# Weight tiles of 1024 columns instead of 512 in a hybrid decoder step

## The chip, the cores and the metric

The kernel runs on one core of one Trainium2 chip. The metric is the device time of one execution in microseconds. A core has five engines that run side by side, each with its own queue in fixed order: TensorE (PE, matrix products; PEld is its weight load), VectorE (DVE), ScalarE (ACT), GpSimd (POOL) and SyncE (SP, which here issues the DMA transfers). They meet through semaphores, and a waiting instruction holds up everything behind it on its engine.

## The reference

One layer of a decoder is computed in fp32 for 1024 prompt tokens and for 8 sample tokens, each of which has a cache of 4096 earlier keys and values in pages of 128. The core of it:

```python
def swiglu(h, w_gate, w_up, w_down):
    return (jax.nn.silu(h @ w_gate) * (h @ w_up)) @ w_down
...
h = x + 0.5 * swiglu(rmsnorm(x, p['ffn1_norm']), p['ffn1_w_gate'], p['ffn1_w_up'], p['ffn1_w_down'])
z = rmsnorm(h, p['mix_norm']) @ p['w_in']
xq, xf, xi, xg, dq, dk, dv = jnp.split(z, IN_SPLITS, axis=-1)
o_hg, s_new = hgrn2_mixer(xq, xf, xi, xg, lb, s0, p['hg_out_norm'])
...
o = jnp.concatenate([o_hg.reshape(B, L, HG_WIDTH), o_da.reshape(B, L, DA_WIDTH)], axis=-1).astype(dt)
h = h + o @ p['w_out']
y = h + 0.5 * swiglu(rmsnorm(h, p['ffn2_norm']), p['ffn2_w_gate'], p['ffn2_w_up'], p['ffn2_w_down'])
```

The model width is 1024, the FFN's inner width 2816. `o_hg` is a gated linear recurrence over chunks of 64 tokens (4 heads), `o_da` an attention of two softmax maps per head (4 heads), for the prompt over itself and for the sample tokens over their cache.

## The kernel before

**Products in three passes.** A product is made at fp32 precision from parts in a faster format: each operand is split into a high part H (the value cast to fp32r) and a low part L (the value less H), and H·H, H·L and L·H are added up in PSUM. So every weight passes through the chain of `split` (L105 and L106): a DMA brings a raw tile `wr` of 512 columns, ScalarE casts it into `wH`, and VectorE, or GpSimd, subtracts to get `wL`. A profile shows all three steps of a weight under L106 (cast and subtraction) and L354 (the load); the tokens' own splits (`xn`, `h`) have L106 too and are told apart by the tile's name.

**Weights in tiles.** The host lays the weights out in blocks of 128 x 512. `wtile` (L359) asks for all that one product needs: two blocks for a gate, up or output matrix of 128 columns (8 row blocks), four for 256 columns of the input projection, and two for 256 columns of the down projection (one in its first block of rows). Raw tiles have 4 buffers, `wH` and `wL` 7 each. `wload` (L350) is issued at a high priority. While the flag `shared[1]` is set, which is from the second token group's first half to the end of the first group's second half, every second tile's low part (`WPOOL`) is subtracted on GpSimd.

**Stages.** The tokens go in two groups of 512 (the sample tokens pass the first half with the first group and the second half with the second). The first group's FFN1 and input projection run alone, then the sample tokens' attention over the cache begins beside them. The second group's first half has the first group's mixer (recurrence, then attention) and the cache attention woven in (`weave`); the first group's second half (output projection, FFN2) has the second group's mixer and the rest of the cache attention; the second group's second half runs alone. In the cache attention each page of keys is loaded (`kv`), multiplied on GpSimd (L954) and reduced on VectorE (L955); each page of values is scaled and added up, for even pages on VectorE (L1004), for odd ones on ScalarE (L1006) and GpSimd (L1008).

**What sets the order.** The code is written in woven order, and a scheduler then sorts every engine's instructions by priorities and by a simulated run. The queues are fixed before the kernel starts. FFN steps that the prediction names: a gate product's result is multiplied by the norm's factor (L399) and, with its tanh, by itself (L402), the up product's result is multiplied in (L409), the factor once more on GpSimd (L411), and the sum is split for the down projection (L431, L433). L402 reads two SBUF tiles in the first group's second half and one SBUF tile and one PSUM bank in the second group's first.

Of the kernel before, what the change touches and what calls it, by code (L numbers as in the profile page):

```python
# [18 lines left out]
P = 128  # L19
# [3 lines left out]
EPS = 1e-6  # L23
# [5 lines left out]
# columns of the constant table  # L29
# [4 lines left out]
def shape_constants():  # L34
# [5 lines left out]
    for l in range(7):  # L40
# [6 lines left out]
        # the columns of right halves alone  # L47
# [12 lines left out]
def kernel(ctx: ExitStack, tc: tile.TileContext, I, O):  # L60
# [74 lines left out]
    def load_consts():  # L135
# [3 lines left out]
        # lower bound: c1n = -(1 - lb) / 2 with lb the softmax over the two rows  # L139
        l0 = DT("wr", [P, 512], bufs=4)  # L140
        l1 = DT("wr", [P, 512], bufs=4)
        SP.dma_start(l0, I["hg_lb_logits"][0:1].broadcast_to([P, 512]))
        SP.dma_start(l1, I["hg_lb_logits"][1:2].broadcast_to([P, 512]))
        mx = DT("wr", [P, 512], bufs=4)
# [8 lines left out]
        # lambda  # L153
        lv = DT("wr", [P, 512], bufs=4)
# [10 lines left out]
        # gains of the mixers  # L165
# [18 lines left out]
    # rows of the sample tokens  # L184
# [15 lines left out]
    class Group:  # L200
        """tokens that pass the weights together: tiles as wide as the group"""
# [9 lines left out]
    class Slice:  # L211
        """columns of a group that one matrix product takes"""
# [53 lines left out]
    def norm_sums(sl):  # L266
        """sums of squares by block, down the partitions; the columns of each height"""
# [6 lines left out]
    def norm_spread(sl, R, r):  # L274
        """the factors along a row, on all partitions"""
# [23 lines left out]
    def scaled(gi, sl, d):  # L299
        """what norm_finish makes, but for the norm's factors: those come with the products' results"""  # L300
# [6 lines left out]
    def norm_row(sl):  # L307
        """the factors alone, along a row"""
# [26 lines left out]
    def xn_pair(w):  # L335
        """room for high and low parts: in one tile, or one each"""
        t = DT("xn", [P, 528], F32R, bufs=17)
        if w <= 264:
            return t[:, 0:w], t[:, 264:264 + w]
        return t[:, 0:w], DT("xn", [P, 528], F32R, bufs=17)[:, 0:w]  # L340
# [9 lines left out]
    def wload(H, L, raw, src):  # L350
        # while DVE has the most to do, some of the low parts on Pool
        shared[0] += 1
        with hp():
            SP.dma_start(raw, src)  # L354
# [4 lines left out]
    def wtile(src, c):  # L359
        """c columns of weights, from tiles of 512 / c blocks of rows: pairs of (high, low) parts"""  # L360
        out = []
        for i in range(src.shape[0]):
            raw = DT("wr", [P, 512], bufs=4)
            H = DT("wH", [P, 512], F32R, bufs=7)
            L = DT("wL", [P, 512], F32R, bufs=7)
            wload(H, L, raw, src[i])
            out += [(H[:, k:k + c], L[:, k:k + c]) for k in range(0, 512, c)]
        return out

    def mm3(ps, W, sl):  # L370
        """ps = W^T x, weights stationary, in three passes"""
# [7 lines left out]
    FB = [2, 4, 4, 4, 4, 4]  # L379

    def ffn(pre, slices, done, deferred=False):
        wg, wu, wd = (I[pre + n] for n in ("_w_gate", "_w_up", "_w_down"))

        def gateup(f, hs):
# [30 lines left out]
            # by slices where what comes before goes by slices  # L415
# [104 lines left out]
    def evac(name, c, ps, tb, kind, row, factors):  # L520
        # of the norm: the factor, half of it, and the eps that it makes of EPS and of 64 EPS
# [15 lines left out]
        else:  # L537
# [9 lines left out]
            with tc.high_priority():  # L547
                if name == "aq":
                    # the scale of the scores over each head's slope comes with the norm
# [6 lines left out]
        # where it goes  # L556
# [15 lines left out]
        else:  # L572
# [3 lines left out]
            # high and low parts side by side, and so below each other once transposed  # L576
# [43 lines left out]
    def hgrn_head(b):  # L620
        """the logarithms of the decays"""
# [8 lines left out]
    def hgrn_block(b):  # L630
# [30 lines left out]
        def stage1(h, q):  # L661
            """decays of four levels (the first of the first half: the running one), and both sides' factors"""
# [19 lines left out]
        def stage2(h, q):  # L682
# [11 lines left out]
            def right(t, l):  # L694
                """the columns of right halves at a level"""
# [72 lines left out]
    def att_scores(h, b, KT):  # L768
        """softmax weights of both maps, combined"""
# [490 lines left out]
```

## Time and profile before

| | |
|---|---|
| Time of the runs | 2474.95 us median of 3 (2472.2 to 2476.01) |
| Profiled execution | span 2471.9 us; no other time of this execution is shown |
| TensorE busy | 2304.7 us, 93% |
| VectorE busy | 1827.5 us, 74% |
| ScalarE busy | 1071.8 us, 43% |
| GpSimd busy | 999.5 us, 40% |
| DMA | 402.37 MB, 163 GB/s mean |

Busy shares are means over stages with different limits, so the table by stretch of time has to be read before any of them means something. An instruction's duration is from its start on the engine to its end; where two engines hinder each other, the one that stands shows a longer duration, not an idle time. So for each instruction its shortest or median duration is to be set against its mean.

### The profile page before, as it was taken

What the parts mean: (1) busy time and instruction counts of PE and PEld (TensorE: products, weight loads), DVE (VectorE), ACT (ScalarE), POOL (GpSimd) and SP (SyncE); (2) the same over time, 40 slices, a digit from 0 to 9 for tenths busy, and PEclk for the clock granted to TensorE, in tenths of its full rate; (3) what the DMA queues carried; (4) which work ended last, traced back from release to release, by engine and by line L of the source; (5) the groups of instructions that cost most, each with busy time, mean ns of one, the idle gap of its engine ahead of it and who ended that gap; (6) DMA issues with size and microseconds to landing.
All of it is one profiled execution on the core that took longest, in us unless ns stands there. A gap on an engine that the chain in (4) does not pass through costs nothing. (4 is left out here: it accounts for less than half of the span.)

```text
span 2471.9 us, 44310 instructions
## 1 busy us (share of the span) xinstructions
PE 2304.7 (93%) x15101; PEld 2079.1 (84%) x15101; DVE 1827.5 (74%) x3750; ACT 1071.8 (43%) x2465; POOL 999.5 (40%) x788
## 2 busy tenths in 40 slices
PE   7999999989998978989899879889798999999999
PEld 6999999989877866767888767677687889999999
DVE  6555657596799796798798997997987766555554
ACT  4322324435544434545554643434465554322222
POOL 4100101381176374474684673785756310100000
PEclk9999999999998998999899999999999999999999
DMA  4332334684466467576785773566755652332332
GB/s 137 90 95 83 112 91 125 183 286 139 130 217 205 134 213 230 165 234 215 239 280 145 243 236 114 186 211 202 235 173 182 183 170 94 90 95 91 90 95 74
DMA packets 273396, 402.37 MB, mean 163 GB/s; under 512 B 29641, under 2 KB 104650, under 8 KB 273170
## 3 DMA queue, kind: packets, MB, share of 16 engines
q1 hardware_dynamic: 273170, 399.54, 52.0%
q8 instruction: 119, 1.95, 0.3%
q14 instruction: 107, 0.88, 0.1%
HBM read 361.22 MB, written 38.21 MB: 162 GB/s over the span
## 5 line engine op out<-in xcount | busy, mean ns | idle before, releaser
L376 PE MATMUL mm<-xn,wH 128*128 128x256 f32 (+2 forms) x4800 | 1121.8, 327 | 19.4 <-DVE xn L106 5.7
L376 PEld LDWEIGHTS mm<-xn,wH 128*128 128x128 f32 x4800 | 808.6, 192 | 94.8 <-DVE xn L106 8.1
L376 PE MATMUL mm<-xn,wL 128*128 128x256 f32 (+2 forms) x2400 | 782.7, 326 | 1.4 <-DVE wL L106 1.4
L106 ACT CAST wH<-wr 128x512 fp32r<-128x512 f32 x672 | 409.3, 617 | 518.1 <-PE mm L376 275.3
L106 DVE TENSOR_TENSOR wL<-wr,wH 128x512 fp32r<-128x512 f32 x504 | 414.7, 825 | 163.8 <-ACT wH L106 132.8
L431 PE MATMUL mm<-h,wH 128*128 128x264 f32 (+2 forms) x2112 | 487.0, 324 | 7.3 <-DVE ft L409 4.7
L376 PEld LDWEIGHTS mm<-xn,wL 128*128 128x128 f32 x2400 | 461.1, 192 | 36.8 <-DVE wL L106 1.8
L954 POOL TENSOR_TENSOR kv<-kv,ss 128x512 f32<-128x512 f32 x256 | 371.2, 1459 | 145.3 <-DMA kv<-in_cache_k 127.1
L431 PEld LDWEIGHTS mm<-h,wH 128*128 128x128 f32 x2112 | 349.9, 190 | 38.4 <-DVE ft L409 5.8
L411 POOL TENSOR_TENSOR ft<-ft,acc 128x256 f32<-128x256 f32 (+1 forms) x110 | 101.5, 922 | 656.6 <-DVE ft L409 645.9
L431 PE MATMUL mm<-h,wL 128*128 128x264 f32 (+2 forms) x1056 | 340.5, 323 | 0.0
L498 PE MATMUL mm<-wH,xn 128*128 128x256 f32 (+1 forms) x1728 | 325.5, 286 | 7.2 <-ACT ez L527 2.5
L106 POOL TENSOR_TENSOR wL<-wr,wH 128x512 fp32r<-128x512 f32 x168 | 237.9, 1417 | 223.0 <-ACT wH L106 184.7
L1004 DVE SCALAR_TENSOR_TENSOR sacc<-kv,sS,sacc 128x128 f32<-128x128 f32 x480 | 283.5, 645 | 20.4 <-POOL sacc L1008 20.4
L498 PEld LDWEIGHTS mm<-wH,xn 128*128 128x128 f32 (+1 forms) x1728 | 259.4, 180 | 17.5 <-ACT ez L527 3.2
L1006 ACT ACTIVATE kv<-kv,sS 128x128 f32<-128x128 f32 x512 | 164.5, 391 | 210.3 <-DMA kv<-in_cache_v 161.2
L498 PE MATMUL mm<-wL,xn 128*128 128x256 f32 (+1 forms) x864 | 246.2, 286 | 1.0 <-DVE wL L106 1.0
L1008 POOL TENSOR_TENSOR sacc<-sacc,kv 128x512 f32<-128x512 f32 x128 | 185.6, 1450 | 117.9 <-issue 27.3
L433 DVE SCALAR_TENSOR_TENSOR xr<-mm,xr 128x264 f32<-128x264 f32 (+2 forms) x288 | 146.0, 511 | 91.4 <-PE mm L431 91.0
L431 PEld LDWEIGHTS mm<-h,wL 128*128 128x128 f32 x1056 | 200.2, 190 | 14.7
L955 DVE TENSOR_REDUCE sS<-kv 128x8 f32<-128x512 f32 x256 | 170.8, 673 | 37.2 <-POOL kv L954 36.8
L498 PEld LDWEIGHTS mm<-wL,xn 128*128 128x128 f32 (+1 forms) x864 | 155.2, 180 | 4.7 <-DVE wL L106 1.2
(219 smaller groups left out, 2409.0 us busy)
## 6 DMA issues: line engine op xcount, KB each, us to landing
kv<-in_cache_k SPq DMA_DIRECT2D x256, 256.0 KB
kv<-in_cache_v SPq DMA_DIRECT2D x256, 256.0 KB
wr<-in_ffn_w_gate SPq DMA_DIRECT2D x176, 256.0 KB
wr<-in_ffn_w_up SPq DMA_DIRECT2D x176, 256.0 KB
wr<-in_ffn_w_down SPq DMA_DIRECT2D x176, 256.0 KB
wr<-in_w_in SPq DMA_DIRECT2D x96, 256.0 KB
aq<-qt SPq DMA_DIRECT2D x64, 128.0 KB
wr<-in_w_out SPq DMA_DIRECT2D x32, 256.0 KB
```

What stands on the lines that cost most here:

```text
L106: return ACT.copy(H, src), (eng or DVE).tensor_tensor(out=L, in0=src, in1=H.bitcast(F32), op=ALU.subtract)
L376: PE.matmul(ps[:, :w], a, b[k][:, :w], start=k == 0 and j == 0, stop=k == n - 1 and j == 2)
L411: POOL.tensor_tensor(out=t, in0=t, in1=sl.acc, op=ALU.mult)
L431: PE.matmul(ps[:, :w], a[:, cs], b[:, :w], start=j == 0 and q == 0, stop=j == m - 1 and q == 2)
L433: DVE.scalar_tensor_tensor(out=sl.xr[d][:, :w], in0=ps[:, :w], scalar=0.25, in1=sl.xr[d][:, :w], op0=ALU.mult, op1=ALU.add)
L498: PE.matmul(ps[:tb, 0:256], a, b, start=k == 0 and j == 0, stop=k == KC - 1 and j == 2)
L954: POOL.tensor_tensor(out=kt, in0=kt, in1=qb, op=ALU.mult)
L955: DVE.tensor_reduce(out=Sb[:, i], in_=kt.rearrange("p (n d) -> p n d", d=64), op=ALU.add, axis=AX.X)
L1004: DVE.scalar_tensor_tensor(out=acc[:, hs], in0=vt[:, hs], scalar=w, in1=acc[:, hs], op0=ALU.mult, op1=ALU.add)
L1006: ACT.activation(vt[:, hs], vt[:, hs], AF.Copy, scale=w)
L1008: POOL.tensor_tensor(out=acc, in0=acc, in1=vt, op=ALU.add)
```

## The change

`wtile` takes the blocks of 512 columns in pairs: one DMA of 128 x 2 x 512 into a raw tile of 1024 columns, one cast and one subtraction over 1024. Where a product needs an odd block (the down projection's first block of rows), half a tile is used. Raw buffers become 2 of 1024, `wH` and `wL` 4 each of 1024. The count for GpSimd's turn (`shared[0]`) goes up once per tile as before, so once per 1024 columns. The few constants that borrow raw buffers take slices of the new ones. Comments are left out in the new file, and with the lines added at L140 and behind L368 later lines stand one, then three further down.

```diff
-        l0 = DT("wr", [P, 512], bufs=4)
-        l1 = DT("wr", [P, 512], bufs=4)
+        l0t = WR()
+        l0 = l0t[:, 0:512]
+        l1 = l0t[:, 512:1024]
...
-        mx = DT("wr", [P, 512], bufs=4)
+        mx = WR()[:, 0:512]
...
-        lv = DT("wr", [P, 512], bufs=4)
+        lv = WR()[:, 0:512]
...
     def wload(H, L, raw, src):
         shared[0] += 1
         with hp():
-            SP.dma_start(raw, src)
+            SP.dma_start(raw.rearrange("p (n c) -> p n c", c=512), src)
             split(H, L, raw, POOL if shared[1] and shared[0] % WPOOL == 0 else DVE)
...
     def wtile(src, c):
         out = []
-        for i in range(src.shape[0]):
-            raw = DT("wr", [P, 512], bufs=4)
-            H = DT("wH", [P, 512], F32R, bufs=7)
-            L = DT("wL", [P, 512], F32R, bufs=7)
-            wload(H, L, raw, src[i])
-            out += [(H[:, k:k + c], L[:, k:k + c]) for k in range(0, 512, c)]
+        for i in range(0, src.shape[0], 2):
+            m = min(2, src.shape[0] - i)
+            raw, H, L = (t[:, 0:512 * m] for t in (WR(), DT("wH", [P, 1024], F32R, bufs=4), DT("wL", [P, 1024], F32R, bufs=4)))
+            wload(H, L, raw, src[i:i + m].rearrange("n p c -> p n c"))
+            out += [(H[:, k:k + c], L[:, k:k + c]) for k in range(0, 512 * m, c)]
         return out
 
+    def WR():
+        return DT("wr", [P, 1024], bufs=2)
```

GpSimd's queue in the second group's first half, where it goes from the third sample token's keys to the fourth's. Numbers behind a name tell buffers apart: `ss512_7978` and `ss512_10261` are the third and the fourth token's queries before, `ss512_7449` and `ss512_9600` after. Before:

```order
L106 TENSOR_TENSOR wL_9740<-wr_9738,wH_9739 128x512
L954 TENSOR_TENSOR kv_10041<-kv_10041,ss512_7978 128x512
L1008 TENSOR_TENSOR sacc_8089<-sacc_8089,kv_9948 128x512
L954 TENSOR_TENSOR kv_10137<-kv_10137,ss512_7978 128x512
L954 TENSOR_TENSOR kv_10188<-kv_10188,ss512_7978 128x512
L106 TENSOR_TENSOR wL_9752<-wr_9750,wH_9751 128x512
L1008 TENSOR_TENSOR sacc_8089<-sacc_8089,kv_10086 128x512
L954 TENSOR_TENSOR kv_10264<-kv_10264,ss512_10261 128x512
```

After:

```order
L106 TENSOR_TENSOR wL_9115<-wr_9113,wH_9114 128x1024
L1011 TENSOR_TENSOR sacc_7548<-sacc_7548,kv_9202 128x512
L957 TENSOR_TENSOR kv_9344<-kv_9344,ss512_7449 128x512
L957 TENSOR_TENSOR kv_9392<-kv_9392,ss512_7449 128x512
L957 TENSOR_TENSOR kv_9482<-kv_9482,ss512_7449 128x512
L1011 TENSOR_TENSOR sacc_7548<-sacc_7548,kv_9305 128x512
L957 TENSOR_TENSOR kv_9533<-kv_9533,ss512_7449 128x512
L957 TENSOR_TENSOR kv_9603<-kv_9603,ss512_9600 128x512
```

Two subtractions of 512 columns that had page products between them have become one of 1024, and the page products stand together behind it.

VectorE's queue in the first group's second half, at the third gate product of the FFN, between the product's result `xt` and its use in L402 (L405 after). Before:

```order
L106 TENSOR_TENSOR h_18509<-ft_18507,h_18508 128x512
L708 COPY_PREDICATED hAT_18788<-masks_17162,my_18789 128x4x16
L399 TENSOR_TENSOR xt_18749<-mm_18724,acc_17352 128x512
L106 TENSOR_TENSOR wL_19211<-wr_19209,wH_19210 128x512
L672 TENSOR_TENSOR hXR_18945<-hE_18940,hqt_18447 128x512
L708 COPY_PREDICATED hAT_18788<-masks_17162,my_18925 128x8x8
L402 SCALAR_TENSOR_TENSOR ft_18721<-ft_18721,xt_18749 128x512
L673 TENSOR_TENSOR hE_18940<-hE_18940,hkT_18460 128x512
```

After:

```order
L676 TENSOR_TENSOR hE_17751<-hE_17751,hkT_17295 128x512
L711 COPY_PREDICATED hAT_17599<-masks_16057,my_17736 128x16x4
L402 TENSOR_TENSOR xt_17560<-mm_17535,acc_16241 128x512
L106 TENSOR_TENSOR wL_17926<-wr_17924,wH_17925 128x1024
L711 COPY_PREDICATED hAT_17599<-masks_16057,my_17736 128x32x2
L970 TENSOR_REDUCE sd8_17634<-nm_17632 8x1
L405 SCALAR_TENSOR_TENSOR ft_17532<-ft_17532,xt_17560 128x512
L711 COPY_PREDICATED hAT_17599<-masks_16057,my_17736 128x64
```

A subtraction of twice the length stands in the same place, the next one of 512 columns, which stood behind the up product's L409 before, is gone, and the steps of the recurrence around it (`hE`, `hXR`, `hAT`) are dealt otherwise.

## Rows read from the trace of the kernel before

**Rows 1.** The page's head.

```profile
span 2471.9 us, 44310 instructions
```

**Rows 2.** Stretches: start:end, length, busy us per engine, TensorE's clock, DMA share, GB/s.

```profile
50.00:480.00 430.00, 428.46 (x3576) 424.42 (x3575) 254.75 (x550) 150.71 (x308) 56.27 (x64) 1.00 0.36 105
480.00:2010.00 1530.00, 1386.10 (x7567) 1172.87 (x7567) 1287.09 (x2609) 744.36 (x1788) 877.03 (x634) 0.95 0.64 199
...
2060.00:2472.00 412.00, 407.39 (x3388) 405.86 (x3387) 224.17 (x448) 127.11 (x251) 35.94 (x47) 1.00 0.29 89
```

**Rows 3.** The sum of the fifteen slices of 50 us that the prediction names.

```profile
sum 750.00, PE 644.04 PEld 531.83 DVE 716.07 ACT 349.15 POOL 554.05; mean PE 42.94 PEld 35.45 DVE 47.74 ACT 23.28 POOL 36.94
```

**Rows 4.** TensorE's waits, 500 to 2050: waiter, releaser, total us, times, longest.

```profile
PE my L744 <- DVE hln L741: 15.3, 11, 4.1
...
PE mm L376 <- DVE wL L106: 1.4, 1, 1.4
```

**Rows 5.** L106 from 100 to 400 us: times, ns min/median/max, first and last start.

```profile
L106 ACT CAST wH<-wr x105: 603/621/627, 99.7 to 399.5; 128x512 fp32r<-128x512 f32 x105
L106 DVE TENSOR_TENSOR wL<-wr,wH x104: 679/693/1299, 100.4 to 399.5; 128x512 fp32r<-128x512 f32 x104
...
L106 ACT CAST h<-ft x35: 399/412/416, 101.2 to 388.9; 128x264 fp32r<-128x264 f32 x18, 128x256 fp32r<-128x256 f32 x17
L106 DVE TENSOR_TENSOR h<-ft,h x35: 415/420/1001, 101.6 to 389.4; 128x264 fp32r<-128x264 f32 x18, 128x256 fp32r<-128x256 f32 x17
```

**Rows 6.** The fifteen slices, writers of `wL` alone: sums on VectorE and on GpSimd.

```profile
sum 750.00, DVE 94.74; mean DVE 6.32
...
sum 750.00, POOL 122.17; mean POOL 8.14
```

**Rows 7.** Groups, 480 to 2010: busy us, mean ns, idle before; one row of line L1004.

```profile
L1004 DVE SCALAR_TENSOR_TENSOR sacc<-kv,sS,sacc 128x128 f32<-128x128 f32 x480 | 283.5, 645 | 20.4 <-POOL sacc L1008 20.4
L106 DVE TENSOR_TENSOR wL<-wr,wH 128x512 fp32r<-128x512 f32 x204 | 183.2, 900 | 20.0 <-ACT wH L106 15.4 <-PE mm L498 4.3 <-DMA ot<-s 0.2
...
L402 DVE SCALAR_TENSOR_TENSOR ft<-ft,xt 128x512 f32<-128x512 f32 x22 | 18.8, 853 | 0.2 <-ACT ft L401 0.2
...
L402 DVE SCALAR_TENSOR_TENSOR ft<-ft,mm 128x512 f32<-128x512 f32 x22 | 14.9, 675 | 0.0
...
L954 POOL TENSOR_TENSOR kv<-kv,ss 128x512 f32<-128x512 f32 x256 | 371.2, 1459 | 145.3 <-DMA kv<-in_cache_k 127.1 <-DVE sacc L1004 2.8 <-DVE hAT L708 2.5
L106 POOL TENSOR_TENSOR wL<-wr,wH 128x512 fp32r<-128x512 f32 x168 | 237.9, 1417 | 223.0 <-ACT wH L106 184.7 <-PE mm L498 23.1 <-PE mm L376 8.6
L1008 POOL TENSOR_TENSOR sacc<-sacc,kv 128x512 f32<-128x512 f32 x128 | 185.6, 1450 | 117.9 <-issue 27.3 <-DVE sacc L1004 18.2 <-ACT kv L1006 17.1
...
L1004 DVE SCALAR_TENSOR_TENSOR sacc<-kv,sS,sacc x480: 333/341/1459, 680.4 to 1892.6; 128x128 f32<-128x128 f32 x160
```

**Rows 8.** Lines L106 and L411 over the span, GpSimd's instructions.

```profile
L106 POOL TENSOR_TENSOR wL<-wr,wH x168: 1261/1312/2187, 636.6 to 1997.7; 128x512 fp32r<-128x512 f32 x168
...
L411 POOL TENSOR_TENSOR ft<-ft,acc x110: 731/752/1792, 38.1 to 2440.1; 128x256 f32<-128x256 f32 x44, 128x264 f32<-128x264 f32 x44, 128x512 f32<-128x512 f32 x22
```

**Rows 9.** The timeline at 1605: start us, duration us, engine, line, instruction.

```profile
1605.48 1.33 POOL L106 TENSOR_TENSOR wL<-wr,wH 128x512 fp32r<-128x512 f32 x1
1605.59 1.76 DVE L402 SCALAR_TENSOR_TENSOR ft<-ft,xt 128x512 f32<-128x512 f32 x1
...
1606.77 1.74 POOL L1008 TENSOR_TENSOR sacc<-sacc,kv 128x512 f32<-128x512 f32 x1
...
1607.28 0.67 DVE L955 TENSOR_REDUCE sS<-kv 128x8 f32<-128x512 f32 x1
```

**Rows 10.** Waits of SP's queue and of GpSimd, 500 to 2050.

```profile
SPq L354 <- POOL wL L106: 123.9, 57, 7.6
...
POOL wL L106 <- ACT wH L106: 184.7, 53, 17.2
```

**Rows 11.** TensorE's timeline at its first dense product; idle before, releaser.

```profile
23.58 0.80 PE L376 MATMUL mm<-xn,wH 128*128 128x256 f32 x2 [1.11 <-ACT xr L101]
```

## The prediction

> **What bounds the kernel now.** I read the span first, then the table of busy time by stretch, then the groups of instructions by line, and last the waits. The span is 2471.9 us [rows 1]. Three stages show in the table by stretch [rows 2]. In 50 to 480 us and again from 2060 us to the end only the dense products of one token group run, and TensorE is busy in 428.46 of 430 us and 407.39 of 412 us, at a granted clock of 1.00, the higher of its two levels. There VectorE, ScalarE and GpSimd have room to spare (VectorE 254.75 and 224.17 us), so nothing that makes the weights' casts cheaper can shorten these stages. [...]
>
> The middle is uneven. I took out the fifteen slices of 50 us in which VectorE is busy 44 us or more (500, 650, 700, 750, 850, 900, 1050, 1250, 1350, 1400, 1450, 1550, 1600, 1700 and 1750). Their sum [rows 3] is the row the argument stands on: of 750 us VectorE is busy 716.07, TensorE only 644.04. So of the 144 us in which TensorE idles in the middle, 106 lie where VectorE is full. In these 750 us I let VectorE's time count one for one; outside them not at all.
>
> TensorE hardly ever waits for weights: 1.4 us once for a low part in the middle, against 15.3 us in 11 waits for a single VectorE step of the recurrence [rows 4]. Prefetch is not what is short.
>
> **The change, part by part.** *Counts.* A weight tile becomes 1024 columns: 672 loads, casts and subtractions become 344, of which 328 are of the double size and 16 (the down projection's first block, two row blocks deep) stay at 512. Bytes, matmuls and the bytes of one descriptor's row (2 KB) stay. Raw buffers go from 4 x 512 to 2 x 1024 (the same bytes), the high and low ones from 7 x 512 to 4 x 1024.
>
> *VectorE's subtraction.* Undisturbed, 512 columns take 693 ns, and the same instruction on 256 to 264 columns takes 420 [rows 5]: 1.08 ns a column. 1024 columns should take 693 + 555 = 1248 ns, so a pair saves 138 ns. [...] The middle has 204 of these [rows 7], 183.2 us; the fifteen slices hold 94.74 us of it [rows 6], about 105 of them, 52 pairs: 52 x 0.138 = 7.2 us off VectorE where it counts.
>
> *ScalarE's cast.* 621 ns for 512 columns, 412 for 256 to 264 [rows 5], so 1046 ns for 1024: a pair saves 0.2 us. ScalarE is busy under half of the middle, so this counts as nothing; were it the bound, the 105 + 86 tiles of the slices would be 96 pairs and 19 us.
>
> *GpSimd's subtraction.* Every second tile of the middle goes there, before and after; before, one half of each gate or up matrix went to VectorE and one to GpSimd, now one whole matrix goes to each in turn. 512 columns take 1312 ns; the product at L411, mostly on 256 to 264 columns, takes 752 [rows 8]: 2.2 ns a column, so 2.45 us for 1024, 0.17 saved per pair.
>
> *What GpSimd does to VectorE.* This is where the price lies. L402 is one instruction with two sources: with both operands in SBUF it takes 853 ns in the middle, with one in PSUM 675 [rows 7]. At 1605.59 such an L402 begins 0.11 us after a GpSimd subtraction of 1.33 us and takes 1.76 us, that is, it stands until GpSimd is done and then runs [rows 9]. The same shows as a mean in the accumulation of the values (L1004: 645 ns in the middle against a median of 341) and in the weights' subtraction (900 against 693). These three groups lose 480 x 0.304 + 204 x 0.207 + 22 x 0.178 = 192 us, against 552 long GpSimd instructions (256 + 168 + 128) in the middle: 0.35 us each, 58 us for the 168 weight ones. After it there are 84 of 2.45 us. At the low end a GpSimd instruction costs VectorE in proportion to its length: 0.35 x 2.45 / 1.31 = 0.65, 55 us in all, 4 fewer. At the high end VectorE is blocked for all of the extra 1.14 us: 1.49 each, 125 us, 67 more. The slices hold 122.17 of the 237.9 us [rows 6, 7], half: from -2 to +33 us. I take the middle, +15: in the example VectorE is stopped at once, but 1.7 us later a reduction (L955) runs in its usual 0.67 us beside a GpSimd instruction of 1.74 [rows 9], so much of VectorE's work goes on.
>
> [...]
>
> *Loads.* Fewer issues on SP's queue cost nothing. SP waits for a raw buffer to come free: 123.9 us in 57 waits on GpSimd's subtraction [rows 10]; behind such a wait stand the page loads of the cache. Half as many waits, each about twice as long: from -5 to +5 us, taken as 0.
>
> *The start.* The first cast needs 512 KB instead of 256. TensorE's first dense product at 23.58 us waits for a copy of the transposed tokens, 1.11 us [rows 11], and not for a weight: nothing. At the 105 GB/s of the first dense stage [rows 2] another 256 KB takes 2.5 us, which is the price if that cover is gone.
>
> **The sum.** +15 - 7 = +8 us on the profiled span: 2479.9. The page gives no time but the span, which lies 3.05 us below the median of the three runs, 2474.95; I keep that difference: **2483 us**.
>
> **The rivals.**
> *Fixed costs win (faster).* If VectorE and GpSimd in the full slices take turns so closely that each waits for the other, what counts is the sum of their lengths, and the waiting does not depend on how the work is cut. Then both savings count: 52 x 0.138 + 43 x 0.17 = 14.5 us, 2460; with the low end of the blocking and GpSimd's saving at nothing, -9 us, 2466. The rows for it are those where GpSimd, too, is long (1.74 us at 1606.77 behind the L402 [rows 9], and 1459 and 1450 ns on average for page products [rows 7]); against it, GpSimd is busy 554.05 of the 750 us [rows 3], so it has room. It decides if fewer than about 2 us of blocking are added in the slices. [...]
>
> *A wash.* The blocking comes to about the 7 us that VectorE saves, or the new interleaving of all queues hides it: 2475, within 5.
>
> *Full blocking (slower still).* Each weight instruction of GpSimd stops VectorE for its whole extra length: +33 - 7 = +26 us, 2501. For it speaks the L402 of [rows 9]; against it, a GpSimd instruction now costs VectorE 0.35 us of its 1.3 to 1.5, about a quarter. [...]
>
> *Weights late (slower).* A whole matrix now hangs on one GpSimd instruction behind page products. GpSimd already waits 184.7 us in 53 waits for a cast [rows 10]. Three tiles lie ready ahead of TensorE; at the dense pace, 430 us for 3576 products [rows 2], a matrix of 48 products lasts 5.8 us, so the cover is 17 us, about what GpSimd's longest wait is (17.2). If ten tiles come 2.45 us late, the time is 2500. Against it: 1.4 us of such waits now, with less cover (seven halves).
>
> The order of the instructions shows that the change does what it says, so that is no rival; but a product's order among the mixer's is dealt anew by the scheduler, and that I can't price beyond single waits such as those of up to 4.1 us in [rows 4].
>
> **How the numbers follow.** The forecast (blocking outweighs, 2480 to 2495) 0.32; fixed costs win (2455 to 2470) 0.31; a wash 0.28; full blocking (2495 to 2506) 0.05; weights late (2495 to 2515) 0.04. Both signs hold much, so the likeliest one's own range is 2480 to 2495. The range for 8 in 10 is 2455 to 2506: it leaves out the tail of the faster case (0.08), that of the late weights (0.02), and what a new interleaving adds on either side (0.08). About 0.2%, 5 us, is what a measurement of this kernel can tell from no change: faster 0.31, same 0.28, slower 0.32 + 0.05 + 0.04 = 0.41.
>
> **What would show it.** VectorE's subtraction of 1024 columns at 1.25 us in the first 450 us, GpSimd's at 2.4 to 2.5. In the middle, VectorE's two-source SBUF instructions: L1004's mean above 645 ns, and single ones of 2.5 us and more, while the PSUM form of L402 stays at 675. VectorE's busy time in the middle near 1287 or above it, although 102 fixed parts (14 us) are gone. The two dense stages stay at 430 and 412 us within 2. I am wrong if L1004's mean falls, if the dense stages change, or if TensorE's waits for wH or wL pass 10 us.

## The result and the profile after

The changed kernel takes 2503.4 us (median of 4 runs, 2501.04 to 2506.26), the kernel before, on the same chip, 2474.08: a ratio of 1.0121 [1.0107, 1.0136], 29 us slower. The forecast was 2483; its range, 2455 to 2506, holds the time near the top end.

The head and the table of busy time of the page of after:

```profile
span 2503.9 us, 42446 instructions
...
PE 2321.4 (93%) x15101; PEld 2087.0 (83%) x15101; DVE 1797.8 (72%) x3504; ACT 1023.3 (41%) x2137; POOL 965.1 (39%) x706
```

The span is 32.0 us above that of [rows 1], although VectorE, ScalarE and GpSimd are all busy for less time than before. TensorE alone is busy longer. To see where, I set the two traces side by side at the same dense product (12,960 of them, in one order in both kernels): product 3300 starts at 427 us before and at 428 after, product 9600 at 2056 and at 2088. The stretch between holds the same dense work, one row from each kernel: start:end, length, busy us of TensorE, its weight loads, VectorE, ScalarE and GpSimd, granted clock, DMA share, GB/s. Before:

```profile
427.00:2056.00 1629.00, 1482.08 (x8314) 1262.21 (x8313) 1345.05 (x2767) 793.02 (x1897) 897.51 (x653) 0.96 0.63 197
```

After:

```profile
428.00:2088.00 1660.00, 1498.21 (x8313) 1269.51 (x8312) 1343.01 (x2655) 766.22 (x1704) 864.30 (x571) 0.95 0.62 193
```

All of the loss is in here: 31 us. TensorE idles 161.8 us instead of 146.9, 15 more, and is busy for 16 us more with the same matmuls, at a lower mean clock. From the granted-clock records of the two traces, outside the start and the end, TensorE is at the lower of the records' two levels (0.5; the higher is 1.0) for 164 us instead of 143, and busy in 142 and 119 us of them. In both traces the median step from one matmul of 512 columns (L376, L379 after) to the next instruction is 427 ns at the lower level and 233 at the higher, so 45 to 50% of that busy time is what the lower level costs: by this estimate 65 to 71 us instead of 54 to 60. So about 15 us are idle time, 10 to 12 the clock, and some 5 I can't assign. The clock's part holds for this pair of executions alone: one of the changed kernel's four had a mean clock of 0.971, that of the profile of before, and took 2501.16 us all the same. VectorE's time is 1343 us against 1345: it did not rise.

The same stretch in pieces cut at the same products, then the last dense stage. Before:

```profile
427.20:1148.00 720.80, 658.02 (x3762) 561.07 (x3760) 582.00 (x1167) 325.06 (x779) 380.71 (x282) 0.96 0.62 195
1148.00:1213.30 65.30, 60.37 (x382) 55.02 (x381) 52.56 (x120) 42.78 (x116) 30.41 (x25) 0.92 0.67 213
1213.30:1389.60 176.30, 158.95 (x1143) 148.69 (x1142) 154.26 (x317) 96.88 (x224) 109.91 (x83) 0.96 0.70 220
1389.60:1579.70 190.10, 166.43 (x833) 136.94 (x832) 172.96 (x316) 85.66 (x193) 120.70 (x84) 0.93 0.60 193
...
1985.80:2056.00 70.20, 68.57 (x452) 61.45 (x451) 43.87 (x117) 38.46 (x88) 6.64 (x8) 1.00 0.54 163
2056.00:2471.00 415.00, 411.39 (x3422) 409.86 (x3420) 226.07 (x453) 128.58 (x253) 35.94 (x47) 1.00 0.29 89
```

After:

```profile
428.00:1156.20 728.20, 661.41 (x3735) 558.03 (x3734) 570.77 (x1089) 305.33 (x671) 368.75 (x248) 0.95 0.62 192
1156.20:1232.10 75.90, 63.03 (x388) 57.51 (x387) 62.10 (x139) 47.52 (x127) 33.84 (x24) 0.90 0.66 200
1232.10:1398.80 166.70, 156.50 (x1152) 148.24 (x1152) 140.36 (x289) 89.15 (x188) 98.39 (x67) 0.98 0.70 217
1398.80:1605.80 207.00, 176.08 (x860) 141.81 (x859) 183.22 (x328) 92.52 (x196) 122.97 (x78) 0.93 0.60 188
...
2010.10:2088.00 77.90, 72.20 (x465) 64.48 (x464) 45.37 (x117) 38.84 (x84) 6.75 (x7) 0.98 0.48 145
2088.00:2503.00 415.00, 411.48 (x3422) 409.64 (x3421) 213.05 (x388) 118.03 (x188) 34.81 (x47) 1.00 0.29 90
```

The last row is the dense stage: 415 us in both, although VectorE has 13 us less to do there. The second and the fourth row are where the kernel falls behind most for their length, by 10.6 and 16.9 us; the third gives 9.6 back. The first and the sixth lose 7.4 and 7.7 us, and the piece left out gives 1.8 back. In the second, VectorE has 139 instructions and 62 us of work where it had 120 and 53; in the third it has 14 us less; in the fourth, where it was 91% busy before, it has 10 us more. The same total, dealt otherwise. More work of VectorE doesn't explain the first row, where it has 11 us less, and hardly the sixth, where it has 1.5 us more.

The groups of after, 480 to 2030 us (busy us, mean ns, idle before), that answer to [rows 7]:

```profile
L1007 DVE SCALAR_TENSOR_TENSOR sacc<-kv,sS,sacc 128x128 f32<-128x128 f32 x480 | 292.7, 663 | 14.0 <-POOL sacc L1011 13.8
L106 POOL TENSOR_TENSOR wL<-wr,wH 128x1024 fp32r<-128x1024 f32 x82 | 206.9, 2523 | 155.8 <-ACT wH L106 115.4 <-PE mm L434 14.6 <-PE my L695 11.6
...
L106 DVE TENSOR_TENSOR wL<-wr,wH 128x1024 fp32r<-128x1024 f32 x102 | 141.0, 1383 | 24.8 <-ACT wH L106 24.5
...
L405 DVE SCALAR_TENSOR_TENSOR ft<-ft,xt 128x512 f32<-128x512 f32 x22 | 18.0, 822 | 0.0
...
L405 DVE SCALAR_TENSOR_TENSOR ft<-ft,mm 128x512 f32<-128x512 f32 x22 | 14.9, 676 | 0.0
```

VectorE's low parts take 141 us where they took 183, yet its sum over the same products is only 2 us lower: other instructions have become dearer, L1007 (L1004 before) by 9 us. From 100 to 400 us, undisturbed (times, ns min/median/max, first and last start), as in [rows 5]:

```profile
L106 ACT CAST wH<-wr x53: 1032/1052/1056, 100.3 to 399.8; 128x1024 fp32r<-128x1024 f32 x53
...
L106 DVE TENSOR_TENSOR wL<-wr,wH x52: 1218/1226/1820, 101.4 to 396.0; 128x1024 fp32r<-128x1024 f32 x52
```

TensorE's waits in the middle of after (waiter, releaser, total us, times, longest):

```profile
PE mx L789 <- DVE atn L791: 20.9, 11, 4.9
PE my L716 <- DVE hAT L711: 15.3, 8, 3.7
...
PE mm L379 <- DVE wL L106: 0.5, 1, 0.5
```

TensorE waits for steps of the attention and the recurrence, and only 0.5 us for a weight. The first two waits were 10.7 and 6.1 us before, and the one that led there, for `hln` [rows 4], has gone from 15.3 to 5.7. Added up over the two stretches from product 3300 to 9600, TensorE's waits for VectorE rose from 113 to 120 us and those for ScalarE from 14 to 26.

### The profile page after: what moved, and what is told of

It is laid out like the page before. It is cut to its first block, busy times and chain, and to the rows that moved or that the text cites. A ratio compares the mean times of both kernels' runs of the same rounds, so it can differ in the third digit from the quotient of the medians.

```text
span 2503.9 us, 42446 instructions
## 1 busy us (share of the span) xinstructions
PE 2321.4 (93%) x15101; PEld 2087.0 (83%) x15101; DVE 1797.8 (72%) x3504; ACT 1023.3 (41%) x2137; POOL 965.1 (39%) x706
## 5 line engine op out<-in xcount | busy, mean ns | idle before, releaser
L379 PE MATMUL mm<-xn,wH 128*128 128x256 f32 (+2 forms) x4800 | 1123.6, 327 | 18.5 <-ACT xn L106 4.6
L379 PEld LDWEIGHTS mm<-xn,wH 128*128 128x128 f32 x4800 | 809.5, 192 | 97.2 <-DVE xn L106 6.0
L379 PE MATMUL mm<-xn,wL 128*128 128x256 f32 (+2 forms) x2400 | 782.7, 326 | 0.5 <-DVE wL L106 0.5
L106 ACT CAST wH<-wr 128x1024 fp32r<-128x1024 f32 (+1 forms) x344 | 352.4, 1026 | 440.8 <-PE mm L379 188.7
L379 PEld LDWEIGHTS mm<-xn,wL 128*128 128x128 f32 x2400 | 461.6, 192 | 37.1 <-DVE wL L106 1.4
L106 DVE TENSOR_TENSOR wL<-wr,wH 128x1024 fp32r<-128x1024 f32 (+1 forms) x258 | 334.4, 1296 | 101.6 <-ACT wH L106 99.7
L414 POOL TENSOR_TENSOR ft<-ft,acc 128x256 f32<-128x256 f32 (+1 forms) x110 | 96.1, 874 | 679.3 <-DVE ft L412 668.9
L1007 DVE SCALAR_TENSOR_TENSOR sacc<-kv,sS,sacc 128x128 f32<-128x128 f32 x480 | 292.7, 663 | 14.0 <-POOL sacc L1011 13.8
L106 POOL TENSOR_TENSOR wL<-wr,wH 128x1024 fp32r<-128x1024 f32 (+1 forms) x86 | 212.2, 2467 | 171.6 <-ACT wH L106 131.2
```

Of the source, the lines that this page charges most:

```text
L106: return ACT.copy(H, src), (eng or DVE).tensor_tensor(out=L, in0=src, in1=H.bitcast(F32), op=ALU.subtract)
L379: PE.matmul(ps[:, :w], a, b[k][:, :w], start=k == 0 and j == 0, stop=k == n - 1 and j == 2)
L414: POOL.tensor_tensor(out=t, in0=t, in1=sl.acc, op=ALU.mult)
L1007: DVE.scalar_tensor_tensor(out=acc[:, hs], in0=vt[:, hs], scalar=w, in1=acc[:, hs], op0=ALU.mult, op1=ALU.add)
```

## The experiments

Four theories were on the table at first. **Length**: GpSimd's longer instruction holds VectorE (the forecast's mechanism at its high end). **Whole matrix**: a matrix hangs on one engine instead of half and half. **Buffers**: fewer, larger ones come and go too coarsely. **Order**: the scheduler, whose simulated times have changed, puts the mixers' steps elsewhere among the dense products. Later, a sharper form of it, **fit**: the kernel before stands in one favourable deal, and any departure costs some 20 us, whatever it is. All times are medians of 4 runs; ratios are to runs of the kernel before on the same chip.

### Cutting the long subtractions where they stand

The finished program of the changed kernel is rewritten: each low-part subtraction of 1024 columns becomes two of 512, directly behind each other. The queues of the other engines are untouched.

```diff
         tile_hymba_step_kernel(tc, ins, outs)
+    in_halves(nc, (mybir.EngineType.Pool,))                          # cut_pool
+    in_halves(nc, (mybir.EngineType.Pool, mybir.EngineType.DVE,))    # cut_both
```

> The changed kernel, every queue in exactly its order, but each of GpSimd's 82 low-part subtractions of 1024 columns of the middle (2.52 us) stands as two of 512 directly behind each other: the first carries the waits, the second the signal. Length theory (VectorE is held for the whole of a long GpSimd instruction, so fewer and longer ones cost the 29 us): VectorE can step in between the halves, at least half of the 29 us comes back, 2475 to 2489, and L1007's mean falls from 663 towards 645. Order theory (the scheduler dealt the queues anew, and the mixers' steps now stand where TensorE waits for them): nothing comes back, 2500 to 2508. Whole-matrix theory (a whole matrix now hangs on one engine) and buffer theory (fewer buffers): also 2500 to 2508.

> As the run before it, but VectorE's 246 subtractions of 1024 columns are cut in two as well, each pair directly behind each other in the changed kernel's order. Length theory: 2478 to 2495, with VectorE's 102 pairs of the middle 14 us longer in busy time, of which at most 7 count. Order, whole-matrix and buffer theories: 2503 to 2512, no better than the changed kernel. VectorE's busy time in all rises by some 30 us (246 x 0.138 = 34) under each.

Cut on GpSimd alone: 2494.71 us, ratio 1.0085 [1.0060, 1.0110]. Cut on both: 2511.65, 1.0160 [1.0136, 1.0184]. The first lies between the ranges of all theories. The difference of its ratio to that of the change is 0.0036, 9 us with an uncertainty of 7. So the length of GpSimd's instructions costs something, some third of the 29 us by the medians, where the length theory asked for half. Its own sign did not come: L1007's mean stays at 665 ns, though its longest falls from 2549 to 1468. Cutting VectorE's, too, costs 17 us again by the medians (uncertain by 9). The row from 480 to 2060 us, with GpSimd's cut alone:

```profile
480.00:2060.00 1580.00, 1421.09 (x7742) 1199.51 (x7740) 1289.77 (x2551) 734.64 (x1638) 873.32 (x637) 0.95 0.62 197
```

and with both cut:

```profile
480.00:2060.00 1580.00, 1423.13 (x7703) 1201.13 (x7701) 1304.23 (x2645) 731.28 (x1630) 868.73 (x636) 0.94 0.62 196
```

These rows cover the same time, not the same work, and the profiled execution of the first kernel was the slowest of its four (2503.1 us). Over the same products, 3300 to 9600, VectorE's time rises by 17.7 us, from 1329.3 to 1347.0, and the stretch grows by 7.6, from 1657.7 to 1665.3. So with the order held, the 17.7 us of VectorE cost 8 us between these two executions and 17 between the medians. Taken together, the long subtractions are 10 us (0.0039, uncertain by 7) better than the short ones in this order. They are not what made the kernel slower.

### The parts, dealt anew

Two kernels take one part of the change each, and the scheduler orders them anew.

```diff
# halves: the changed kernel, but
-            split(H, L, raw, POOL if shared[1] and shared[0] % WPOOL == 0 else DVE)
+            ACT.copy(H, raw)
+            for k in range(0, H.shape[1], 512):
+                s = slice(k, k + 512)
+                (POOL if shared[1] and k else DVE).tensor_tensor(out=L[:, s], in0=raw[:, s], in1=H[:, s].bitcast(F32), op=ALU.subtract)
# whole: the kernel before, but
-            split(H, L, raw, POOL if shared[1] and shared[0] % WPOOL == 0 else DVE)
+            split(H, L, raw, POOL if shared[1] and (shared[0] - 1) // 2 % WPOOL == 1 else DVE)
```

> The changed kernel's tiles, loads, casts and buffers of 1024 columns, but the low part is written as two subtractions of 512 columns, in the middle one on VectorE and one on GpSimd as in the kernel before, and the scheduler orders it all anew. Length theory and whole-matrix theory: 2470 to 2482, as before the change. Buffer theory: 2498 to 2508. Order theory: a third deal, anywhere from 2465 to 2515, with the dense stages as they were and the difference in a few places of the middle.

> The kernel before with its tiles, loads, casts, subtractions and buffers of 512 columns; only in the middle two tiles in a row go to VectorE and the next two to GpSimd, so that a whole gate or up matrix is split by one engine, as in the changed kernel. Whole-matrix theory: 2495 to 2510. Length theory and buffer theory: 2470 to 2480. Order theory: another deal, 2465 to 2515, and then the place of the loss is not that of the changed kernel.

halves: 2498.72, 1.0111 [1.0084, 1.0138]. whole: 2492.68, 1.0080 [1.0056, 1.0103]. Length falls again: without any long subtraction both are over 20 us slower than the kernel before. Buffers could explain the first but not the second, which has the buffers of before; a whole matrix on one engine could nearly explain the second but not the first. Of the four, only order allows both, and its range was wide enough to allow almost anything, so it had to be tested by itself.

### The order exchanged

Here all instructions but the weights' own (load, cast, subtraction) are tied to a given order on each engine; the scheduler only puts the weights' instructions between them. kept_all is the changed kernel in the order of before, swapped the kernel before in the order of the changed one, kept_pe holds TensorE alone. The edit, shortened:

```diff
         tile_hymba_step_kernel(tc, ins, outs)
+        for e, place in ORDER.items():       # the other kernel's order, engine by engine
+            todo = [i for i in nc.cur_bb.bb.instructions if i.engine == e and i.name not in weights]
+            for a, b in zip(place, place[1:]):
+                tc.add_manual_dep(todo[b], todo[a].name, info, reason="order")
```

> The other way round: the kernel before, with all its tiles, loads, casts, subtractions and buffers of 512 columns, but all other instructions held on each engine in the order that the changed kernel has. Order theory: the loss is here without any tile of 1024 columns, 2493 to 2510, at the same products as in the changed kernel. Length, whole-matrix and buffer theories: 2466 to 2482, as the kernel before.

> The changed kernel (tiles, loads, casts, subtractions and buffers of 1024 columns), but all other instructions (14465 matmuls, 3150 of VectorE, 1680 of ScalarE, 616 of GpSimd, 1050 transfers) are held on each engine in the order that the kernel before has; the scheduler only puts the weights' own instructions between them. Order theory: the 29 us are gone, 2464 to 2480, and what is left against the kernel before is the fixed parts saved (up to 7 us) and the blocking. Length, whole-matrix and buffer theories: 2495 to 2510, since everything they speak of is still there.

> As the run that holds the order of before on all engines, but held on TensorE alone; VectorE, ScalarE, GpSimd and the transfers are dealt anew. If the place of the mixers' products among the dense ones is what counts: 2464 to 2482. If it is the order on VectorE (whose steps TensorE waits for): 2485 to 2505. Length, whole-matrix and buffer theories: 2495 to 2510.

swapped: 2505.48, 1.0135 [1.0116, 1.0153]. With tiles, casts, subtractions and buffers of 512 columns, and with the order alone, the kernel loses all that the change loses. Most of it is lost at the same products; only the first 7 us of the changed kernel, before product 6300, are not. Its rows for the second, fourth and sixth piece of the table above:

```profile
1147.80:1225.70 77.90, 62.96 (x389) 57.48 (x388) 61.40 (x144) 48.97 (x135) 34.18 (x28) 0.90 0.63 195
...
1393.70:1604.50 210.80, 178.68 (x859) 145.92 (x858) 186.92 (x338) 94.31 (x216) 126.77 (x89) 0.91 0.59 186
...
2011.30:2087.90 76.60, 70.96 (x465) 63.00 (x464) 47.12 (x124) 40.31 (x95) 6.74 (x8) 1.00 0.50 151
```

What stands there can be seen on two tiles: `ap`, the attention's combined weights, and `sacc`, the accumulated values of the cache rows. VectorE's instructions on `ap` in the second piece and on `sacc` in the fourth, before:

```profile
1148.00:1213.30 65.30, 4.69 (x8) 0.92 0.67 213
...
1389.60:1579.70 190.10, 34.04 (x64) 0.93 0.60 193
```

in the changed kernel:

```profile
1156.20:1232.10 75.90, 7.89 (x14) 0.90 0.66 200
...
1398.80:1605.80 207.00, 41.58 (x76) 0.93 0.60 188
```

and in swapped:

```profile
1147.80:1225.70 77.90, 9.39 (x14) 0.90 0.63 195
...
1393.70:1604.50 210.80, 39.89 (x76) 0.91 0.59 186
```

14 steps of the attention instead of 8 beside the one run of dense products, 76 of the cache rows instead of 64 beside the other. In the second piece one pair of waits is the same in both kernels. In the changed kernel, VectorE's first and TensorE's 1.4 us behind it:

```profile
DVE ap L801 <- ACT ap L800: 6.2, 3, 5.4
...
PE nm L984 <- DVE tiny L198: 4.7, 1, 4.7
```

in swapped:

```profile
DVE ap L800 <- ACT ap L799: 7.3, 2, 6.5
...
PE nm L983 <- DVE tiny L197: 4.1, 1, 4.1
```

The kernel before has only the first there, and hardly waits in it:

```profile
DVE ap L798 <- ACT ap L797: 0.4, 1, 0.4
```

So the order of the changed kernel is enough to make the loss, and in that order its larger tiles add nothing that can be told from no change.

But kept_all, in the order of before, does not get it back: 2506.74, 1.0132 [1.0115, 1.0149], against 2464 to 2480 expected of the order theory and 2495 to 2510 of the other three, which held here and failed for swapped. Nor does kept_pe: 2519.22, 1.0189 [1.0172, 1.0206], outside of what any theory expected, with TensorE in the order of before and the steps that it waits for dealt anew. So the order of before is good only with the tiles of before. The tiles make no difference in the order of the changed kernel (1.0135 and 1.0121) and 33 us in that of before. No cost that belongs to a tile by itself does that, and the theory had to be sharpened to that of the fit. It says how the times lie and not by which step they arise.

### A deal for its own sake

If the fit is what counts, changes that add no work must be as dear.

```diff
# redeal: the kernel before; redeal_1024: the changed kernel
-    R0, R1 = 0.55, 0.8
+    R0, R1 = 0.56, 0.8
# more_bufs: the kernel before, with one buffer more each
-            H = DT("wH", [P, 512], F32R, bufs=7)
-            L = DT("wL", [P, 512], F32R, bufs=7)
+            H = DT("wH", [P, 512], F32R, bufs=8)
+            L = DT("wL", [P, 512], F32R, bufs=8)
```

> The kernel before with one number changed: in the first woven stage the mixer's steps are written at 0.56 of the dense work's pace instead of 0.55. Tiles, instructions and buffers are the same, the scheduler deals the middle anew. Order theory: the time moves by more than its measurement is uncertain, by up to some 30 us either way, 2450 to 2505. Length, whole-matrix and buffer theories: 2470 to 2480.

> The changed kernel with the one number of the earlier run (0.56 for 0.55): a third order in which tiles of 512 columns, 2507 us, and of 1024 can be compared, after that of before (2473 and 2507) and that of the changed kernel (2505 and 2503). If tiles of 1024 columns cost something of their own, 10 us or more: 2517 to 2530. Fit theory: no sign of the tiles, 2490 to 2515.

> The kernel before, all tiles of 512 columns, with eight buffers for the high and eight for the low parts instead of seven (the bytes that the changed kernel gives them); the scheduler deals anew. Buffer theory (less room ahead of TensorE is what costs): no slower than the kernel before, 2460 to 2478. Fit theory (what counts is that the deal is not the one the kernel's numbers were set for): slower in spite of the room, 2483 to 2510.

redeal: 2507.03, 1.0139 [1.0122, 1.0156]. One pace, changed by 0.01, costs 34 us, as much as the whole change or more, and 2 us above what was expected of the order theory. more_bufs: 2496.86, 1.0099 [1.0082, 1.0115]: more room, and 24 us slower, which the buffer theory cannot give. redeal_1024: 2494.14, 1.0081 [1.0049, 1.0113]: with this number the tiles of 1024 columns are the faster ones, by 0.0058, 14 us (uncertain by 9).

### The pieces, with the order of before held

The last two take kept_all apart: the low parts go back to 512 columns on the engines that they had before (kept_halves), then the casts as well (kept_loads), so that only loads and buffers are those of the change. The edits, shortened; `shared[2]` counts the halves:

```diff
 # as kept_all, and
+            parts = [slice(k, k + 512) for k in range(0, H.shape[1], 512)]
-            ACT.copy(H, raw)
+            [ACT.copy(H[:, s], raw[:, s]) for s in parts]     # kept_loads alone
+            for s in parts:                                   # both
+                (POOL if shared[1] and shared[2] % WPOOL == 0 else DVE).tensor_tensor(out=L[:, s], in0=raw[:, s], in1=H[:, s].bitcast(F32), op=ALU.subtract)
```

> As the run that holds all other instructions in the order of before on all engines (2507 us), with loads, casts and buffers of 1024 columns, but the low part in two subtractions of 512 columns, each on the engine that it has in the kernel before. VectorE then makes the second half some 2 of its instructions earlier than before the change, not 9. Pull-ahead and blocking theory (one long subtraction on VectorE or GpSimd is what costs when the order is kept): 2474 to 2488. Buffer and load theory (fewer, larger raw tiles come and go more coarsely): 2498 to 2510. Fit theory (any departure from the one deal that the kernel's numbers were set for costs some 20 us or more, whatever it is): 2490 to 2510.

> As the run before it, but the casts, too, are of 512 columns; only the loads and the buffers (2 raw, 4 high, 4 low tiles of 1024) are those of the change. Pull-ahead and blocking theory: 2470 to 2480. If the cast of 1.03 us is what costs: this one at 2475 and the one before it at 2495 or above. Buffer and load theory: 2498 to 2510, as with all of the change. Fit theory: 2485 to 2510.

kept_halves: 2503.89, 1.0122 [1.0088, 1.0155]. kept_loads: 2496.07, 1.0091 [1.0059, 1.0123]. The pull-ahead theory (a long subtraction does early what could have waited) falls with the first. The first is inside the ranges of the buffer theory and of the fit. The second is inside that of the fit and 2 us below that of the buffers, which its uncertainty of 8 us covers, so neither run decides between these two. With 14,465 matmuls and all other work in the order of before, and every cast and subtraction of 512 columns, the kernel is 23 us slower, because loads and buffers are coarser or because the weights' instructions stand elsewhere (by 2 places in the mean on VectorE, ScalarE and GpSimd, by up to 46).

### All of them at the same products

Worked out from the traces: how many us later than in the kernel before the n-th dense product starts.

```
product  before us  after  swapped  whole  redeal  more_bufs  kept_all  kept_loads
3300      427.2      0.8     0.1     0.5     0.8      1.2        0.1       1.4
6300     1148.0      8.2    -0.2    -0.5    -2.4     -3.2       10.5       7.4
6600     1213.3     18.8    12.4     4.4     7.8      3.7        9.5       7.2
7500     1389.6      9.2     4.1     1.6     8.0     -2.0        8.5       4.0
8100     1579.7     26.1    24.8    14.0    25.0      7.9       17.0       7.3
9300     1985.8     24.3    25.5    13.6    37.3     24.4       32.7      11.8
9600     2056.0     32.0    31.9    21.5    34.4     22.5       35.7      15.3
last     2466.1     32.0    32.0    21.5    34.4     22.5       35.7      15.2
```

The traces are of single executions; that of kept_loads was the fastest of its four, 7 us under their median. Outside the woven middle nothing moves in any of these by more than 1.5 us. In it, all fall behind between products 7500 and 8100, where VectorE is 91% busy in the kernel before, and five of the seven between 6300 and 6600. I had expected of whole that a new deal would lose in other places; it loses in the same ones, by less. So it seems to be the kernel before that is unusually good there.

| Kernel | us | ratio | TensorE idle in the span, us | mean clock |
|---|---|---|---|---|
| before | 2474.08 | 1 | 167 | 0.971 |
| after | 2503.40 | 1.0121 | 183 | 0.964 |
| cut_pool | 2494.71 | 1.0085 | 186 | 0.969 |
| cut_both | 2511.65 | 1.0160 | 187 | 0.965 |
| halves | 2498.72 | 1.0111 | 188 | 0.975 |
| whole | 2492.68 | 1.0080 | 182 | 0.968 |
| swapped | 2505.48 | 1.0135 | 186 | 0.964 |
| kept_all | 2506.74 | 1.0132 | 187 | 0.963 |
| kept_pe | 2519.22 | 1.0189 | 200 | 0.965 |
| redeal | 2507.03 | 1.0139 | 187 | 0.967 |
| redeal_1024 | 2494.14 | 1.0081 | 180 | 0.971 |
| more_bufs | 2496.86 | 1.0099 | 182 | 0.970 |
| kept_halves | 2503.89 | 1.0122 | 180 | 0.966 |
| kept_loads | 2496.07 | 1.0091 | 175 | 0.969 |

Idle is the span less TensorE's busy time, from each page. The mean clock is over the whole trace: the trace of before has no clock record for its first 27.9 us, where those of after and swapped show 17.1 us at the lower level, and about half of the step from 0.971 to 0.964 is that. Each group of runs had its own runs of the kernel before beside it (medians of 2471 to 2474 us), so the ratios are what can be compared. None of the thirteen beats the kernel before; the nearest is 0.8% slower.

**What stays open.** Why the deal of before is some 20 us better than every other one tried. Its TensorE idles least (167 us against 175 to 200) and is busy least (2304.7 us against 2308.9 to 2322.1), and no single wait accounts for that. That its paces were picked with just these tiles would explain it, but no run here shows how it came to be. Nor was the tile of 1024 columns tried with paces of its own beyond 0.56; whether some deal of it beats 2474 us is not known. A kernel with 1024 columns in which the weights' instructions, too, stand exactly where they stood before was not tried, nor one with coarser loads and buffers and everything else in its place. So in the order of before the coarser loads and buffers stand as a rival to the fit for the 23 us of kept_loads.

## Why the prediction was right or wrong

**The sign and the range held, the reason did not.** Slower had the largest chance, 0.41, and 2503 is inside 2455 to 2506. But the 8 us of the forecast were VectorE's, and VectorE's time over the same products went from 1345 to 1343 us. That 2503 falls inside the range, 3 us under its upper end, is luck: what made it had no term in the sum.

**Where it is decided: right.** All of the loss lies in the woven middle; the dense stage at the end takes 415.0 us in both, and TensorE waits 0.5 us for a low part.

**VectorE's subtraction: the price about right, its use not settled.** 1226 ns for 1024 columns against 1248 forecast and 693 for 512 [rows 5], so a pair saves 160 ns and not 138: my line through two shapes of [rows 5], the smaller one of mixed widths, came out 22 ns too long. The term counted 7.2 us, half of the middle. Cut in place, VectorE's fixed parts cost 17 us by the medians and 8 between the profiled executions, for 17.7 us of busy time: somewhere between the half that the forecast took and all of it.

**GpSimd's blocking: there, but not at its high end.** GpSimd's subtraction of 1024 columns takes 2.41 us in the median (forecast 2.45). The form of L405 with an operand in PSUM stays at 676 ns, and single steps of L1007 of 2.5 us came, as forecast. In the four kernels whose GpSimd subtracts 1024 columns at once (after, redeal_1024, kept_all, kept_pe), 27 to 30 of the 480 steps take over 1.6 us; in the ten others none takes over 1.54. The mean was no sign: it is 663 ns (645 before), but 665 with GpSimd's cut in two and 596 in swapped, which has the tiles of before. The line over the span of after (times, ns min/median/max, first and last start):

```profile
L1007 DVE SCALAR_TENSOR_TENSOR sacc<-kv,sS,sacc x480: 328/341/2549, 685.3 to 1931.8; 128x128 f32<-128x128 f32 x160
```

and the timeline at its longest one (start and duration in us; three of L1007 in one row):

```profile
1898.67 4.12 DVE L1007 SCALAR_TENSOR_TENSOR sacc<-kv,sS,sacc 128x128 f32<-128x128 f32 x3 [0.71 <-POOL sacc L1011]
...
1898.94 2.40 POOL L106 TENSOR_TENSOR wL<-wr,wH 128x1024 fp32r<-128x1024 f32 x1 [0.31 <-ACT wH L106]
```

Three steps with a median of 0.34 us take 4.12, one of them 2.55, while GpSimd's subtraction runs for 2.40: less that median the one of 2.55 stood for 2.21 us, nearly all of it. But cutting GpSimd's instructions in two gives 9 us back (uncertain by 7): the 15 of the term is not excluded, the 33 of its high end is.

**The sum of the two: the wrong sign.** +15 - 7 was +8; by the ratios of cut_both and of the change it is -10 (uncertain by 7) in the changed kernel's order, and by the medians of the two cuts +9 - 17. The rival "fixed costs win" was right on what the long subtractions do directly, and the forecast's own mechanism, blocking outweighs, fell.

**Full blocking** gave 2501 and so the right time for a wrong reason: the length of GpSimd's instructions accounts for some 9 of the 29 us (uncertain by 7). **Weights late** fell with the 0.5 us. **A wash** fell.

**Loads at nothing: not upheld, not refuted.** kept_loads is 23 us slower with nothing but coarser loads and buffers and their places, but more_bufs is as slow with finer ones and more room. SP's waits for GpSimd's subtraction went from 123.9 us in 57 to 84.7 in 36, the longest from 7.6 to 12.5: fewer, but not twice as long in the mean, as forecast (2.2 and 2.4 us). What they cost by themselves was not isolated.

**The step that failed** is the sentence that the scheduler deals the products anew among the mixer's, "and that I can't price beyond single waits such as those of up to 4.1 us in [rows 4]". It was given 0.08 at the range's two ends. It was the largest term of the sum: in the runs a new deal without any tile of 1024 columns costs 20 to 34 us (whole, more_bufs, swapped, redeal). A bound on its size could be read: the middle held 144 us of idle TensorE [rows 2], 111 of it in waits for VectorE, and a new deal sets all of them anew; in the runs TensorE's idle time moved by 8 to 33 us, and its busy time by 4 to 17 with it. I had seen that the order changes and had put the term at zero.

## What to carry to other kernels

Where a list scheduler orders the queues, a change of a size is two changes, the direct one and a new deal: run a null change (one pace moved by a hundredth, one buffer more) to see what a deal alone is worth, and hold the order, both ways, to see which of the two moved the time. Here a deal was worth 20 to 34 us and the longer subtractions some 10 the other way (uncertain by 7), so nothing is settled for or against the larger tile until the numbers that set the order have been chosen for it too. When the local prices of a forecast come true and their sum doesn't, compare the two traces at the same products: where an engine's total is the same and one stretch holds more of its work than before, that shows an order, not a price. And name a sign by what only the mechanism can make: the longest steps told the long subtractions apart in all fourteen kernels, the mean did not.

## What the runs showed of the hardware

Idle time did not come alone: of the 31 us lost in the middle between the two traces, 15 were idle and 16 were the same matmuls running longer, 10 to 12 of these, by the estimate above, from more time at the lower of the two clock levels (164 us instead of 143). In the piece where the kernel gained (1232 to 1399 us) it went the other way, idle time down from 17.4 to 10.2 us and the granted clock up from 0.96 to 0.98. The costs of the tiles themselves held no surprise: the cast takes 1052 ns for 1024 columns against 621 for 512, the subtraction 1226 on VectorE against 693.
